# Mixer of a Trainium2 backbone layer: S5 scans of a pair of groups in one scan per direction, and mixer products moved from GpSimd to VectorE

## The chip, the core and the metric

The kernel runs on one core of one Trainium2 chip. The metric is the device time of one execution in microseconds (us), the median of several runs.

## What is computed

The program is one layer of a diffusion backbone: a half-step SwiGLU feed-forward block, a mixer, and a second feed-forward block, on 1024 latent tokens of width 1024 with 256 context tokens as a prefix. The change is in the mixer. There the width is split: one half goes through a gated short convolution on a grid, the other through a bidirectional S5 state-space scan, and both halves go into one output projection. The S5 part has 32 groups with 64 complex states each, in two directions. Cut to what matters:

```python
def s5_scan(ug, lam_bar, b_bar, h0, reverse):
    bu = jnp.einsum('blgh,gph->blgp', ug.astype(jnp.complex64), b_bar)
    first = bu.shape[1] - 1 if reverse else 0
    bu = bu.at[:, first].add(lam_bar * h0)
    a = jnp.broadcast_to(lam_bar, (1,) + bu.shape[1:])
    _, h = lax.associative_scan(_linear_recurrence, (a, bu), axis=1, reverse=reverse)
    return h
...
    st_c = s5_states(u_c, disc, (zero, zero))          # context tokens
    h0s = (st_c[0][:, -1], st_c[1][:, 0])
    p = modulate(rms_norm(x, mix_g_pre[i]), mods[3], mods[4]) @ w_in[i]
    bg, cg, v, u = jnp.split(p, splits, axis=-1)
    y_conv = bg * grid_short_conv(cg * v, conv_w[i])
    y_ssm = s5_readout(u, s5_states(u, disc, h0s), disc, ssm_d[i], w_glu[i], b_glu[i])
    y = jnp.concatenate([y_conv, y_ssm], axis=-1) @ w_out[i]
```

## The kernel before

The tokens of a sequence are taken in 128 chunks of 8 (CL = 128), so that a recurrence over 1024 tokens becomes one over 128 chunk states, and what lies inside a chunk is matrix products on TensorE. The 32 groups are worked in 16 pairs by the generator `s5_pair` (L1428 on); text below counts them from 0 to 15. The states of the forward direction stand on partitions 0 to 63, those of the backward direction on partitions 64 to 127.

For one pair the steps are these. TensorE forms the chunk inputs in PSUM (tiles `bt`, two groups, real and imaginary part, 128 latent chunks and 32 context chunks each). VectorE multiplies the context part with a table (four products of 128x64), adds and subtracts them, and sums them up to the start state (two reductions, written to column 0 or 127 of tile `w`). It then multiplies the latent part with a table of rotations (four products of 128x256 into `p1` and `p2`), and adds and subtracts (two of 128x256). The rotation makes the recurrence a real one with a coefficient `r8` that is constant for each state. So there are four real sequences of a direction (two groups, real and imaginary), and VectorE runs eight scans of 64x127, each with a start value taken from a column of `w`. At last the rotation is undone: two products of 128x512 and two sums of 128x256, which the kernel before gives to GpSimd (`pl`). The result `q1` is the operand of the pair's readout, matrix products that TensorE adds into the PSUM tiles `yps` of four pairs.

Around the pairs runs `cover`: units of the convolution branch (`conv`: twelve column blocks of `w_in`, each projected by 2 x 24 matrix products of 128x512) and of `out_conv`. The loop in `run` starts the chunk inputs of pair a+1, the VectorE part of pair a, some units of cover by the list `UNITS`, and the readout of pair a-1. The exact order on each engine is made by the scheduler at build time; each engine then works its list strictly in order. A projection in fp32 precision is three products of a high and a low part of the weights, which are split by `wcols` and `split` (L157): ScalarE writes the high part, a second engine subtracts it. The tables `PC` and `V0` say which of the convolution's splits and products go to GpSimd:

```python
nxt = self.wcols(win, seq[p + 1], nc.gpsimd if PC[p % len(PC)] else None)
...
if n == 2 and V0[j] or n == 1 and V1[j]:
    h_ = self.t2()
    nc.scalar.activation(h_, pt, AF.Copy)
    self.mul(t[:, cs], t[:, cs], h_, nc.gpsimd)
else:
    self.mul(t[:, cs], t[:, cs], pt)
```

Since GpSimd takes its operand from SBUF here, ScalarE copies the product out of PSUM first. After four pairs `s5_out` writes their readout to DRAM (`yd`), gathers it in eight loads and runs the gelu on it, on VectorE and ScalarE. Scratch tiles of the mixer come from a ring of twelve (`t2`).

Of the kernel before, what the change touches and what calls it, by code (L numbers as in the profile page):

```python
# [12 lines left out]
AF = mybir.ActivationFunctionType  # L13
OP = mybir.AluOpType
AX = mybir.AxisListType

P = 128
# [11 lines left out]
CL = NT // T8  # L29
# [39 lines left out]
class Kernel:  # L69
# [110 lines left out]
    def setup(self):  # L180
        nc, i = self.nc, self.i
        self.cp = self.pool("cp")
        self.dr = self.pool("dr", space=bass.MemoryType.DRAM)
        self.psum = self.pool("psum", bufs=8, space=bass.MemoryType.PSUM)
        self.sm = self.pool("sm", bufs=8)
        self.wp = self.pool("wp", bufs=6)
        self.tp = self.pool("tp", bufs=1)
        self.tb = self.t(self.tp, [P, 5 * D], "tb")
        self.ring([self.tb[:, D * k : D * k + D] for k in range(5)])
        self.wrs = [self.t(self.wp, [P, D], f"wr{k}", bufs=1) for k in range(4)]  # L190
        self.zp = self.pool("zp", bufs=32)

        dr = self.dr
        self.x1d = self.t(dr, [T8, CL, D], "x1d")
        self.x2d = self.t(dr, [T8, CL, D], "x2d")
        self.rowd = [self.t(dr, [KT, P], f"rowd{k}") for k in range(4)]
        self.pd = self.t(dr, [PAIRS, P, TO], "pd")
        self.pwd = self.t(dr, [P, D], "pwd")
        self.brd = self.t(dr, [P, D], "brd")
        self.gd = self.t(dr, [H, G, 15, H], "gd")  # L200
        self.td = self.t(dr, [P, G, P], "td")
        self.ud = self.t(dr, [G * H, T8, CL], "ud")
        self.ucd = self.t(dr, [G * H, T8, CC], "ucd")
        self.yd = self.t(dr, [T8, H, G, CL], "yd")
        self.zd = [self.t(dr, [P, NT], f"zd{k}") for k in range(4)]
        self.t2d = [self.t(dr, [P, 512], f"t2d{k}") for k in range(NF // 2)]
        self.scd = [self.t(dr, [P, 4 * NC], f"scd{k}") for k in range(6)]
        self.sd = [[self.t(dr, [P, NT], f"sd{n}_{k}") for k in range(NF)] for n in range(2)]

        cp = self.cp  # L210
        rows = self.t2([16, P])
        self.load(rows[0:8, :], i["c"][0].rearrange("(k p) -> k p", p=P))
        self.load(rows[8:16, :], i["c_ctx"].rearrange("(k p) -> k p", p=P))
        self.ident = self.t(cp, [P, P], "ident")
        make_identity(self.tc.nc, self.ident)
        srow = self.t2([16, P])
        nc.scalar.activation(srow, rows, AF.Silu)
        pt = self.ps()
        self.tr(pt[:, :16], srow, 16)
        self.scol = self.t(cp, [P, 16], "scol")  # L220
        nc.vector.tensor_copy(self.scol, pt[:, :16])
        self.ones = self.t(cp, [P, 1], "ones")
        nc.gpsimd.memset(self.ones, 1.0)
        self.modc = {}

    def selector(self):

        nc, cp = self.nc, self.cp
        red = self.t(cp, [P, 32], "red")
        nc.vector.tensor_reduce(  # L230
            red, self.ident.rearrange("p (a j) -> p j a", j=32), axis=AX.X, op=OP.add
        )
        self.sel = self.t(cp, [P, P], "sel")
        for a in range(4):
            nc.vector.tensor_copy(self.sel[:, 32 * a : 32 * a + 32], red)
# [1192 lines left out]
    def s5_pair(self, a, u, yps):  # L1428

        nc, pl = self.nc, self.nc.gpsimd  # L1430
        fw, bw = slice(0, 64), slice(64, 128)
        pa, pb = self.z([P, EO]), self.z([P, EO])
        self.load(pa, self.pd[a, :, :EO])
        self.load(pb[:, : TO - EO], self.pd[a, :, EO:])
        self.load(
            pb[:, TO - EO : PW - EO].rearrange("p (q n) -> p q n", q=2), self.td[:, 2 * a : 2 * a + 2, :]
        )
        yield
        us = [u[:, 2 * a + q, :] for q in range(2)]
        bm = lambda q, r: pa[:, BO + 256 * r + P * q : BO + 256 * r + P * q + P]  # L1440
        tab = lambda o, n: pb[:, o - EO : o - EO + 2 * n].rearrange("p (q c) -> p q c", q=2)
        bt = [self.ps()[:, : 2 * (CL + CC)].rearrange("p (r c) -> p r c", r=2) for _ in range(2)]
        for q in range(2):
            for r in range(2):
                nc.tensor.matmul(bt[q][:, r, :], bm(q, r), us[q], start=True, stop=True)

        hs = self.t2([P, 2, 2, 2, CC])
        shp = [P, 2, CC]
        for r in range(2):
            for q in range(2):  # L1450
                self.mul(
                    hs[:, r, q], bt[q][:, :, CL:], tab(FO + 64 * r, CC)[:, q].unsqueeze(1).to_broadcast(shp)
                )
        self.sub(hs[:, 0, :, 0], hs[:, 0, :, 0], hs[:, 1, :, 1])
        self.add(hs[:, 0, :, 1], hs[:, 0, :, 1], hs[:, 1, :, 0])
        w = self.t2([P, 2, 2, CL])
        for r, c in ((fw, 0), (bw, CL - 1)):
            nc.vector.tensor_reduce(w[r, :, :, c : c + 1], hs[r, 0], axis=AX.X, op=OP.add)

        shp = [P, 2, 2, CL]  # L1460
        er, ei = (tab(EO + 256 * r, CL) for r in range(2))
        p1, p2 = self.t2(shp), self.t2(shp)
        for q in range(2):
            for p, e in ((p1, er), (p2, ei)):
                self.mul(p[:, q], bt[q][:, :, :CL], e[:, q].unsqueeze(1).to_broadcast([P, 2, CL]))
        er, ei = (e.unsqueeze(2).to_broadcast(shp) for e in (er, ei))
        self.add(p1[:, :, 0], p1[:, :, 0], p2[:, :, 1])
        self.sub(p1[:, :, 1], p1[:, :, 1], p2[:, :, 0])
        n = CL - 1
        for q in range(2):  # L1470
            for r in range(2):
                for d, z, o, c in ((fw, slice(0, n), slice(1, CL), 0), (bw, slice(n, 0, -1), slice(n - 1, None, -1), n)):
                    r8 = self.r8[d, 2 * a + q : 2 * a + q + 1].to_broadcast([64, n])
                    nc.vector.tensor_tensor_scan(
                        w[d, q, r, o], r8, p1[d, q, r, z], w[d, q, r, c : c + 1], op0=OP.mult, op1=OP.add
                    )
        q1 = self.t2(shp)
        self.mul(q1, w, er, pl)
        self.mul(w, w, ei, pl)
        self.sub(q1[:, :, 0], q1[:, :, 0], w[:, :, 1], pl)  # L1480
        self.add(q1[:, :, 1], q1[:, :, 1], w[:, :, 0], pl)
        yield
        if not yps:
            yps.extend(self.ps() for _ in range(2))
        for q in range(2):
            o = yps[q][:, (a % 4) * CL : (a % 4) * CL + CL]
            t0 = TO - EO + P * q
            nc.tensor.matmul(o, pb[:, t0 : t0 + P], us[q][:, :CL], start=True, stop=False)
            for r in range(2):
                c0 = CO + 256 * r + P * q  # L1490
                nc.tensor.matmul(o, pa[:, c0 : c0 + P], q1[:, q, r, :], start=False, stop=r == 1)
        yield
# [26 lines left out]
    def conv(self, hi, lo, yc):  # L1519
# [5 lines left out]
        for p, c0 in enumerate(seq):  # L1525
# [5 lines left out]
            for h in range(2):  # L1531
# [3 lines left out]
                if h == 0 and p + 1 < len(seq):  # L1535
                    nxt = self.wcols(win, seq[p + 1], nc.gpsimd if PC[p % len(PC)] else None)
                if n == 0:
                    nc.scalar.activation(cv[:, cs], pt, AF.Copy)
                else:
                    t = cv if n == 1 else o  # L1540
                    if n == 2 and V0[j] or n == 1 and V1[j]:
                        h_ = self.t2()
# [70 lines left out]
    def run(self):  # L1613
# [41 lines left out]
        go = lambda tokens: [act[c]() for c in tokens]  # L1655
        go(S0)
        ab = (self.modc[1, 0], self.modc[0, 0])
# [357 lines left out]


PP = PH = PU = 0
PC = (0, 1, 0, 0, 1, 0, 1, 1, 0, 1, 1, 1)
FIVE = 4
S0 = 'lffllfllflllllll'  # L2020
S1 = 'wahhaahaahafPpaaqwhafpahpwhwhhwqqqqqqqqqqqqpqqqqPeePhhhPhhhhehPhhpewwhhhPPPphPwhhehPh'
S2 = 'hhhhhhhhhhhhpphhppppphp'
X2A = (0, 2)
FW3 = 18
V0 = (1, 1, 0, 0)
V1 = (0, 0, 0, 0)
UNITS = (5, 0, 0, 2, 0, 0, 1, 1, 2, 0, 2, 1, 1, 0, 3, 1, 0, 0, 6)

# [58 lines left out]
```

## Time and profile before

| | us |
|---|---|
| median of 3 runs (2123.9 to 2125.89) | 2124.05 |
| the profiled execution's own time | 2125.93 |
| its span, first to last instruction | 2124.2 |
| busy: TensorE (PE) | 1925.3 (91%) |
| busy: VectorE (DVE) | 1636.0 (77%) |
| busy: ScalarE (ACT) | 817.0 (38%) |
| busy: GpSimd (POOL) | 229.5 (11%) |

The profile is one execution, so the shares are averages over stages with different limits. The mixer's scans lie between 1122.4 and 1299.7 us of the span. The profile of this kernel names line 51 for nearly every instruction, since a helper records them all, so groups are told apart by the tiles that they write and read: `ps` is PSUM, `t` a scratch tile of the ring, `wr` a raw weight block and `w` its split, `z` a larger tile.

### The profile page before, as it was taken

What the parts mean: (1) busy time and instruction counts of PE and PEld (TensorE: products, weight loads), DVE (VectorE), ACT (ScalarE), POOL (GpSimd) and SP (SyncE); (2) the same over time, 40 slices, a digit from 0 to 9 for tenths busy, and PEclk for the clock granted to TensorE, in tenths of its full rate; (3) what the DMA queues carried; (4) which work ended last, traced back from release to release, by engine and by line L of the source; (5) the groups of instructions that cost most, each with busy time, mean ns of one, the idle gap of its engine ahead of it and who ended that gap; (6) DMA issues with size and microseconds to landing.
All of it is one profiled execution on the core that took longest, in us unless ns stands there. A gap on an engine that the chain in (4) does not pass through costs nothing.

```text
span 2124.2 us, 25468 instructions
## 1 busy us (share of the span) xinstructions
PE 1925.3 (91%) x9018; PEld 1594.7 (75%) x9018; DVE 1636.0 (77%) x2813; ACT 817.0 (38%) x1416; POOL 229.5 (11%) x136
## 2 busy tenths in 40 slices
PE   5779998898899988999997779998899999998997
PEld 4568776686899866877886668886688888886876
DVE  6689998998766699598549998478875555579867
ACT  5433322333343333566531113347233333333543
POOL 0000000041337100000003552010000000000000
PEclk9889999999999999999999899999899999999999
DMA  8347552344579969367684433233552322267754
GB/s 299 95 145 245 160 184 84 88 150 139 172 241 264 320 226 339 128 229 279 186 235 174 153 127 114 72 104 114 182 175 79 99 80 90 70 226 250 243 169 168
DMA packets 338444, 366.21 MB, mean 172 GB/s; under 512 B 43216, under 2 KB 250764, under 8 KB 338316
## 3 DMA queue, kind: packets, MB, share of 16 engines
q1 hardware_dynamic: 336012, 356.19, 51.6%
q10 hardware_dynamic: 2304, 8.39, 1.0%
q8 instruction: 71, 1.16, 0.2%
q14 instruction: 57, 0.47, 0.1%
HBM read 299.22 MB, written 67.35 MB: 173 GB/s over the span
## 4 chain that ended last, share of the span: by engine, by line
PE 54%; DVE 29%; DMA 8%; issue 4%; ACT 2%; POOL 2%; SPq 1%; DVEq 0%; ACTq 0%; POOLq 0%
PE ps L51 54%; DVE t L51 10%; DVE z L51 6%; DVE w L51 5%; DVE tb L51 5%; DMA wr<-in_ffn_w_down 2%; DMA tb<-in_w_ada 2%; POOL z L51 1%; SPq L51 1%; DMA wr<-in_ffn_w_gu 1%; DMA z<-in_w_ada 1%; ACT z L51 1%; ACT w L51 1%; DMA wr<-t2d 1%; ACT t L51 0%
## 5 line engine op out<-in xcount | busy, mean ns | idle before, releaser
L51 PE MATMUL ps<-z,w 128*128 128x512 f32 (+1 forms) x5712 | 1245.9, 379 | 94.4 <-ACT w L51 46.1
L51 PEld LDWEIGHTS ps<-z,w 128*128 128x128 f32 x5712 | 1020.8, 194 | 296.1 <-ACT w L51 52.5
L51 PE MATMUL ps<-w,w 128*128 128x512 f32 x1848 | 439.3, 397 | 29.9 <-DVE w L51 23.9
L51 PEld LDWEIGHTS ps<-w,w 128*128 128x128 f32 x1848 | 348.4, 191 | 117.5 <-DVE w L51 35.0
L51 ACT ACTIVATE w<-wr 128x512 fp32r<-128x512 f32 (+1 forms) x308 | 228.9, 747 | 378.8 <-PE ps L51 287.0
L51 DVE TENSOR_TENSOR w<-wr,w 128x512 fp32r<-128x512 f32 (+1 forms) x302 | 268.6, 894 | 91.1 <-ACT w L51 83.6
L51 ACT ACTIVATE w<-t 128x512 fp32r<-128x512 f32 x264 | 160.2, 626 | 294.0 <-DVE t L51 255.6
L51 DVE TENSOR_TENSOR w<-t,w 128x512 fp32r<-128x512 f32 x264 | 181.1, 699 | 40.9 <-ACT w L51 40.6
L51 DVE TENSOR_TENSOR t<-t,ps 128x512 f32<-128x512 f32 x150 | 102.2, 683 | 66.0 <-PE ps L51 65.6
L51 ACT ACTIVATE w<-z 128x512 fp32r<-128x512 f32 x132 | 83.3, 631 | 161.1 <-PE ps L51 158.4
L51 DVE TENSOR_TENSOR w<-z,w 128x512 fp32r<-128x512 f32 x132 | 90.8, 688 | 48.0 <-ACT w L51 47.8
L51 ACT ACTIVATE t<-ps 128x512 f32<-128x512 f32 (+2 forms) x135 | 73.7, 548 | 99.7 <-PE ps L51 98.0
L51 DVE TENSOR_TENSOR z<-z,z 128x512 fp32r<-128x512 f32 (+3 forms) x127 | 103.8, 852 | 9.6 <-ACT z L51 5.8
L51 DVE SCALAR_TENSOR_TENSOR tb<-tb,scol 128x1024 f32<-128x1024 f32 x77 | 97.9, 1280 | 8.6 <-DMA tb<-in_w_ada 8.4
L51 DVE TENSOR_TENSOR t<-wr 128x512 f32<-128x512 f32 x126 | 85.4, 685 | 16.7 <-DMA wr<-in_ffn_w_gu 11.1
L51 POOL TENSOR_TENSOR z<-z,z 128x1024 f32<-128x1024 f32 x24 | 85.4, 3576 | 76.4 <-PE ps L51 39.8
L51 ACT ACTIVATE t<-z 128x1024 bf16<-128x1024 f32 (+3 forms) x132 | 75.2, 605 | 44.3 <-DVE z L51 32.1
L51 ACT ACTIVATE t<-t 128x512 f32<-128x512 f32 (+1 forms) x81 | 50.6, 625 | 104.1 <-DVE t L51 100.1
L51 PE MATMUL ps<-z,t 128*128 128x512 f32 x384 | 87.8, 389 | 1.1 <-ACT t L51 1.1
L51 PEld LDWEIGHTS ps<-z,t 128*128 128x128 f32 x384 | 72.0, 188 | 16.4 <-ACT t L51 1.5
L51 POOL TENSOR_TENSOR tb<-tb 128x512 f32<-128x512 f32 x24 | 33.8, 1422 | 451.3 <-DVE w L51 431.0
L51 ACT ACTIVATE z<-z 128x512 fp32r<-128x512 f32 (+2 forms) x76 | 47.9, 672 | 78.6 <-DVE z L51 72.5
(124 smaller groups left out, 1447.6 us busy)
## 6 DMA issues: line engine op xcount, KB each, us to landing
wr<-in_ffn_w_gu SPq DMA_DIRECT2D x156, 512.0 KB, 4.1
wr<-in_ffn_w_down SPq DMA_DIRECT2D x242, 256.0 KB, 4.4
tb<-in_w_ada SPq DMA_DIRECT2D x64, 512.0 KB, 5.0
sd<-z SPq DMA_DIRECT2D x44, 512.0 KB, 4.8
z<-sd SPq DMA_DIRECT2D x88, 256.0 KB, 5.6
z<-in_w_ada SPq DMA_DIRECT2D x24, 512.0 KB, 6.1
wr<-in_ffn_w_down SPq DMA_DIRECT2D x22, 512.0 KB, 3.6
wr<-in_w_in SPq DMA_DIRECT2D x20, 512.0 KB, 4.0
```

What stands on the lines that cost most here:

```text
L51: r = f(*a, **kw)
```

## The change

The four sequences of a direction are laid end to end in one row of 516 columns, 129 for each sequence: a start state and 128 inputs. A coefficient tile `co` holds `r8` in every column but those between two sequences, where it holds 0, so that one scan runs through all four and begins anew at each. There are now two scans of 64x515 in a pair, one for each direction. ScalarE writes `co` for each pair, out of a constant `mask`, in two instructions of 128x258 and 128x259. The four operations after the scan go from GpSimd to VectorE. With `PC` and `V0` zero, six weight splits and four products of the convolution go to VectorE too, and the four copies out of PSUM on ScalarE that fed those products are gone. A pair takes six scratch tiles (`hs`, `pp`, `w`, `co`, `p2`, `q1`) and no longer five.

```diff
--- before.py
+++ after.py
@@ -222,6 +222,9 @@
         self.ones = self.t(cp, [P, 1], "ones")
         nc.gpsimd.memset(self.ones, 1.0)
         self.modc = {}
+        self.mask = self.t(cp, [P, 2 * CL + 3], "mask")
+        nc.gpsimd.memset(self.mask, 1.0)
+        nc.gpsimd.memset(self.mask[:, :: CL + 1], 0.0)
 
     def selector(self):
 
@@ -1453,32 +1456,39 @@
                 )
         self.sub(hs[:, 0, :, 0], hs[:, 0, :, 0], hs[:, 1, :, 1])
         self.add(hs[:, 0, :, 1], hs[:, 0, :, 1], hs[:, 1, :, 0])
-        w = self.t2([P, 2, 2, CL])
-        for r, c in ((fw, 0), (bw, CL - 1)):
-            nc.vector.tensor_reduce(w[r, :, :, c : c + 1], hs[r, 0], axis=AX.X, op=OP.add)
-
+
+
+        n = CL + 1
+        pp, w, co = self.t2([P, SW]), self.t2([P, SW]), self.t2([P, SW])
+        for q in range(2):
+            nc.scalar.activation(
+                co[:, 2 * n * q : 2 * n * (q + 1) + q], self.mask[:, : 2 * n + q], AF.Copy,
+                scale=self.r8[:, 2 * a + q : 2 * a + q + 1],
+            )
+        seg = lambda v, c: v[:, c : c + 4 * n].rearrange("p (q r c) -> p q r c", q=2, r=2)
+        for d, c in ((fw, 0), (bw, n)):
+            nc.vector.tensor_reduce(seg(pp, 0 if c == 0 else 1)[d, :, :, c - (c > 0) : c + (c == 0)], hs[d, 0], axis=AX.X, op=OP.add)
         shp = [P, 2, 2, CL]
         er, ei = (tab(EO + 256 * r, CL) for r in range(2))
-        p1, p2 = self.t2(shp), self.t2(shp)
+        p1, p2 = seg(pp, 0)[:, :, :, 1:], self.t2(shp)
         for q in range(2):
             for p, e in ((p1, er), (p2, ei)):
                 self.mul(p[:, q], bt[q][:, :, :CL], e[:, q].unsqueeze(1).to_broadcast([P, 2, CL]))
         er, ei = (e.unsqueeze(2).to_broadcast(shp) for e in (er, ei))
         self.add(p1[:, :, 0], p1[:, :, 0], p2[:, :, 1])
         self.sub(p1[:, :, 1], p1[:, :, 1], p2[:, :, 0])
-        n = CL - 1
-        for q in range(2):
-            for r in range(2):
-                for d, z, o, c in ((fw, slice(0, n), slice(1, CL), 0), (bw, slice(n, 0, -1), slice(n - 1, None, -1), n)):
-                    r8 = self.r8[d, 2 * a + q : 2 * a + q + 1].to_broadcast([64, n])
-                    nc.vector.tensor_tensor_scan(
-                        w[d, q, r, o], r8, p1[d, q, r, z], w[d, q, r, c : c + 1], op0=OP.mult, op1=OP.add
-                    )
-        q1 = self.t2(shp)
-        self.mul(q1, w, er, pl)
-        self.mul(w, w, ei, pl)
-        self.sub(q1[:, :, 0], q1[:, :, 0], w[:, :, 1], pl)
-        self.add(q1[:, :, 1], q1[:, :, 1], w[:, :, 0], pl)
+        nc.vector.tensor_tensor_scan(
+            w[fw, 1 : 4 * n], co[fw, : 4 * n - 1], pp[fw, : 4 * n - 1], 0.0, op0=OP.mult, op1=OP.add
+        )
+        nc.vector.tensor_tensor_scan(
+            w[bw, 4 * n - 1 : 0 : -1], co[bw, 4 * n : 1 : -1], pp[bw, 4 * n : 1 : -1], 0.0, op0=OP.mult, op1=OP.add
+        )
+        w = seg(w, 1)[:, :, :, :CL]
+        q1, q2 = self.t2(shp), p2
+        self.mul(q1, w, er)
+        self.mul(q2, w, ei)
+        self.sub(q1[:, :, 0], q1[:, :, 0], q2[:, :, 1])
+        self.add(q1[:, :, 1], q1[:, :, 1], q2[:, :, 0])
         yield
         if not yps:
             yps.extend(self.ps() for _ in range(2))
@@ -2015,14 +2025,15 @@
 
 
 PP = PH = PU = 0
-PC = (0, 1, 0, 0, 1, 0, 1, 1, 0, 1, 1, 1)
+PC = (0,)
 FIVE = 4
+SW = 520
 S0 = 'lffllfllflllllll'
 S1 = 'wahhaahaahafPpaaqwhafpahpwhwhhwqqqqqqqqqqqqpqqqqPeePhhhPhhhhehPhhpewwhhhPPPphPwhhehPh'
 S2 = 'hhhhhhhhhhhhpphhppppphp'
 X2A = (0, 2)
 FW3 = 18
-V0 = (1, 1, 0, 0)
+V0 = (0, 0, 0, 0)
 V1 = (0, 0, 0, 0)
 UNITS = (5, 0, 0, 2, 0, 0, 1, 1, 2, 0, 2, 1, 1, 0, 3, 1, 0, 0, 6)
 
```

In the built order this is what stands on VectorE for pair 3, from its first product to its scans (`ps_9386` and `ps_9387` are its chunk inputs; the built program names a scan SCALAR_TENSOR_TENSOR). Before:

```order
L51 TENSOR_TENSOR t_1449_9392<-ps_9386,z_9271 128x64
L51 TENSOR_TENSOR t_1449_9392<-ps_9387,z_9271 128x64
L51 TENSOR_TENSOR t_1449_9392<-ps_9386,z_9271 128x64
L51 TENSOR_TENSOR t_1449_9392<-ps_9387,z_9271 128x64
L51 TENSOR_TENSOR t_1449_9392<-t_1449_9392 128x2x32 x2
L51 TENSOR_REDUCE t_1450_9399<-t_1449_9392 64x4 x2
L51 TENSOR_TENSOR t_1451_9402<-ps_9386,z_9271 128x256
L51 TENSOR_TENSOR t_1452_9403<-ps_9386,z_9271 128x256
L51 TENSOR_TENSOR t_1451_9402<-ps_9387,z_9271 128x256
L51 TENSOR_TENSOR t_1452_9403<-ps_9387,z_9271 128x256
L51 TENSOR_TENSOR t_1451_9402<-t_1451_9402,t_1452_9403 128x2x128 x2
L51 SCALAR_TENSOR_TENSOR t_1450_9399<-r_91_175,t_1450_9399,t_1451_9402 64x127 x8
```

With the change, from the two scans of the pair ahead (`ps_9376` and `ps_9377` are now pair 3's chunk inputs, `t_1440` is the `q1` of pair 2):

```order
L51 SCALAR_TENSOR_TENSOR t_1437_9284<-t_1438_9285,t_1436_9283 64x515 x2
L51 TENSOR_TENSOR t_1440_9299<-t_1437_9284,z_9217 128x512
L51 TENSOR_TENSOR t_1439_9290<-t_1437_9284,z_9217 128x512
L51 TENSOR_TENSOR t_1451_9382<-ps_9376,z_9266 128x64
L51 TENSOR_TENSOR t_1451_9382<-ps_9377,z_9266 128x64
L51 TENSOR_TENSOR t_1451_9382<-ps_9376,z_9266 128x64
L51 TENSOR_TENSOR t_1451_9382<-ps_9377,z_9266 128x64
L51 TENSOR_TENSOR t_1440_9299<-t_1440_9299,t_1439_9290 128x2x128 x2
L51 TENSOR_TENSOR t_1451_9382<-t_1451_9382 128x2x32 x2
L51 TENSOR_REDUCE t_1452_9389<-t_1451_9382 64x4 x2
L51 TENSOR_TENSOR t_1452_9389<-ps_9376,z_9266 128x2x128
L51 TENSOR_TENSOR t_1455_9396<-ps_9376,z_9266 128x256
```

The two products of the pair ahead stand directly behind its scans, its two sums behind the first four products of pair 3, and the eight scans are two.

On TensorE this is the place of pair 13's readout before (`ps_10309` and `ps_10310` are the readout's PSUM tiles, `t_1563` and `t_1574` the `q1` of pairs 12 and 13, `ps_10322` a chunk input of pair 14, `ps_10361` a unit of the convolution with 24 products):

```order
L51 MATMUL ps_10309<-t_1563_10151,z_10035 128x128 x2
L51 MATMUL ps_10310<-tb_72,z_10036 128x128
L51 MATMUL ps_10310<-t_1563_10151,z_10035 128x128 x2
L51 MATMUL ps_10309<-tb_72,z_10115 128x128
L51 MATMUL ps_10309<-t_1574_10213,z_10114 128x128 x2
L51 MATMUL ps_10310<-tb_72,z_10115 128x128
L51 MATMUL ps_10322<-tb_72,z_10176 128x160 x2
L51 MATMUL ps_10323<-tb_72,z_10176 128x160 x2
L51 MATMUL ps_10361<-z_7420,w_10273 128x512 x2
L51 MATMUL ps_10361<-z_7420,w_10274 128x512
```

With the change the readout of pair 13 reads `t_1585`, and stands here (`ps_10311` is that unit of the convolution, of which the last products are shown, `ps_10348` and `ps_10349` are the chunk inputs of pair 15):

```order
L51 MATMUL ps_10311<-z_7429,w_10227 128x512
L51 MATMUL ps_10311<-z_7430,w_10226 128x512 x2
L51 MATMUL ps_10311<-z_7430,w_10227 128x512
L51 MATMUL ps_10348<-tb_72,z_10270 128x160 x2
L51 MATMUL ps_10262<-t_1585_10166,z_10073 128x128
L51 MATMUL ps_10263<-t_1585_10166,z_10073 128x128
L51 MATMUL ps_10349<-tb_72,z_10270 128x160 x2
```

The first half of pair 13's readout moved from before the convolution's 24 products to behind them, and behind the chunk inputs of pair 14 and half of those of pair 15.

On ScalarE the coefficient tiles stand between other work; `t_1558` to `t_1583` are those of pairs 11 to 13, with the mixer's own steps around them:

```order
L51 ACTIVATE z_8494<-z_8497 128x1024
L51 ACTIVATE z_8494<-z_8494 128x1024
L51 ACTIVATE t_1558_10017<-mask_175,r_92_178 128x258
L51 ACTIVATE t_1558_10017<-mask_175,r_92_178 128x259
L51 ACTIVATE t_1571_10093<-mask_175,r_92_178 128x258
L51 ACTIVATE t_1571_10093<-mask_175,r_92_178 128x259
L51 ACTIVATE w_10337<-wr_2_73 128x1024
L51 ACTIVATE z_10119<-ps_9917 128x4x128
L51 ACTIVATE z_10119<-ps_9918 128x4x128
L51 ACTIVATE t_1583_10152<-mask_175,r_92_178 128x258
L51 ACTIVATE t_1583_10152<-mask_175,r_92_178 128x259
```

Four coefficient instructions stand behind the two steps on `z_8494`, which belong to the gelu of the second four pairs; before, nothing on VectorE's scans depended on ScalarE's list.

## Rows read from the trace of the kernel before

**Rows 1.** The page: span, and busy time of three engines with share and instructions.

```profile
span 2124.2 us, 25468 instructions
...
PE 1925.3 (91%) x9018; PEld 1594.7 (75%) x9018; DVE 1636.0 (77%) x2813; ACT 817.0 (38%) x1416; POOL 229.5 (11%) x136
```

**Rows 2.** Engines by stretch: the scans, and what follows; columns in the first line.

```profile
core 0: us, PE busy (x) PEld busy (x) DVE busy (x) ACT busy (x) POOL busy (x), PEclk, DMA share, GB/s
1122.40:1299.70 177.30, 139.43 (x687) 118.53 (x687) 169.36 (x382) 26.31 (x43) 87.90 (x69) 0.90 0.39 131
...
1310.00:1373.30 63.30, 63.30 (x280) 52.08 (x278) 34.82 (x52) 26.73 (x47) 0.00 (x0) 1.00 0.34 108
```

**Rows 3.** Waits, 1122.4 to 1299.7: us in total, times, longest.

```profile
PE ps L51 <- POOL t L51: 26.6, 8, 7.7
...
PE ps L51 <- DVE t L51: 5.1, 2, 3.6
...
DVE z L51 <- DMA z<-yd: 1.3, 1, 1.3
```

**Rows 4.** The chain that ended last, around the last stall: start, us, what.

```profile
1270.58 0.49 DVE t L51
...
1271.14 1.27 POOL t L51
...
1272.48 2.32 POOL t L51
...
1278.12 21.96 PE ps L51 x105
```

**Rows 5.** VectorE by shape, 1122.4 to 1299.7: xcount, busy us, mean ns, idle before.

```profile
L51 DVE TENSOR_TENSOR_SCAN t<-r,t,t 64x127 f32<-64x127 f32 x128 | 63.5, 496 | 1.6
...
L51 DVE TENSOR_TENSOR t<-t,t 128x256 f32<-128x256 f32 x32 | 20.9, 693 | 0.5
L51 DVE TENSOR_TENSOR t<-t 128x64 f32<-128x64 f32 x32 | 15.1, 512 | 0.5
...
L51 DVE SCALAR_TENSOR_TENSOR z<-z,cols,z 128x1024 f32<-128x1024 f32 x3 | 5.3, 1762 | 1.3 <-DMA z<-yd 1.3
L51 DVE TENSOR_TENSOR z<-z,ps 128x512 f32<-128x512 f32 x6 | 4.0, 681 | 0.1
L51 DVE SCALAR_TENSOR_TENSOR z<-z,cols,z 128x960 f32<-128x960 f32 x2 | 3.9, 1954 | 0.0
L51 DVE TENSOR_TENSOR w<-wr,w 128x1024 fp32r<-128x1024 f32 x2 | 3.5, 1767 | 0.0
```

**Rows 6.** VectorE in order of time, pairs 14 and 15: start, us, instructions.

```profile
1283.87 0.36 DVE L51 TENSOR_TENSOR t<-t 128x64 f32<-128x64 f32 x2
...
1286.39 0.76 DVE L51 TENSOR_TENSOR t<-t,t 128x256 f32<-128x256 f32 x2
...
1291.67 0.90 DVE L51 TENSOR_TENSOR t<-t 128x64 f32<-128x64 f32 x2
...
1294.67 1.18 DVE L51 TENSOR_TENSOR t<-t,t 128x256 f32<-128x256 f32 x2
```

**Rows 7.** VectorE by shape, whole span.

```profile
L51 DVE TENSOR_TENSOR t<-z,z 128x512 f32<-128x512 f32 x44 | 30.0, 685 | 0.1
...
L51 DVE SCALAR_TENSOR_TENSOR z<-z,sy,tb 128x1024 f32<-128x1024 f32 x24 | 29.8, 1283 | 0.3
...
L51 DVE TENSOR_TENSOR z<-wr,z 128x1024 fp32r<-128x1024 f32 x8 | 9.6, 1220 | 0.7 <-ACT z L51 0.7
...
L51 DVE TENSOR_TENSOR tb<-tb 128x64 f32<-128x64 f32 x16 | 3.4, 222 | 0.2
```

**Rows 8.** TensorE in order of time, around the last stall.

```profile
1276.46 0.80 PE L51 MATMUL ps<-t,z 128*128 128x128 f32 x2 [7.68 <-POOL t L51]
...
1281.08 6.37 PE L51 MATMUL ps<-z,w 128*128 128x512 f32 x24
```

**Rows 9.** GpSimd in order of time: its work of pairs 13 and 14.

```profile
1271.14 3.66 POOL L51 TENSOR_TENSOR t<-t,z 128x512 f32<-128x512 f32 x2 [3.80 <-DVE t L51]
...
1291.07 2.66 POOL L51 TENSOR_TENSOR t<-t,z 128x512 f32<-128x512 f32 x2 [9.78 <-DVE t L51]
```

**Rows 10.** ScalarE by shape, whole span: an activation near the size of a coefficient instruction.

```profile
L51 ACT ACTIVATE t<-ps 128x256 f32<-128x256 f32 x26 | 9.4, 367 | 2.5 <-PE ps L51 2.5
```

## The prediction

> **What bounds the kernel now.** I read the page first. TensorE is busy for 91% of the span and VectorE for 77% [rows 1], so over the whole program TensorE comes first. The change lies in one stage, so I then took the engines by stretch. Between 1122.4 and 1299.7 us, the stretch of the sixteen pairs, VectorE is busy for 169.4 of 177.3 us and TensorE for only 139.4, so TensorE stands idle for 37.9 us; between 1310 and 1373.3 us it is TensorE that is busy all the time [rows 2]. VectorE sets the pace of the scans, and TensorE that of what follows. Third come the waits of that stretch: TensorE waits longest for GpSimd, 26.6 us in eight waits, since its readout of a pair needs the four GpSimd operations behind the scans; it waits 5.1 us for VectorE's tiles, and VectorE itself hardly waits, 1.3 us for the gather of `yd` [rows 3]. Last the chain of the end: it runs through VectorE's scans up to 1271.07 us, then 7 us through GpSimd's operations of pair 13, and at 1278.12 us passes to TensorE, which works on from there [rows 4]. So a microsecond saved ahead of 1278 counts if it brings pair 13's readout forward; one saved behind it on VectorE or GpSimd is hidden under TensorE.
>
> **The scans.** The 128 scans of 64x127 take 63.5 us, 496 ns each [rows 5]. No row shows a scan of 515 columns. From below: one that costs as an ordinary product does, where 512 columns take 685 ns and 64 take 222, that is 1.03 ns a column and 156 ns fixed [rows 7]; the 388 columns more then bring a scan to 496 + 388 x 1.03 = 0.90 us. From above: nothing is fixed and all of the 496 ns goes with the columns, 3.9 ns each, 2.01 us. Between them I take the parts. Fixed are 156 ns, and a column operand costs some 60 more (1283 against 1220 ns for 1024 columns with and without it [rows 7]). This leaves 280 ns for 127 columns, 2.2 ns each, and 515 columns with 156 ns make 1.29 us. All 32 come to 41.3 us: 22.2 us less than before.
>
> [...]
>
> **The products.** Each pair gives VectorE two products of 128x512 at 685 ns [rows 7] and two sums of 128x256, which took 0.76 us together where GpSimd was idle [rows 6]: 2.13 us, 34.1 us for the 16. In both orders they stand behind the pair's own scans, so this lies on VectorE's path, with no cover.
>
> **The convolution's part.** Five splits fall into the stretch (the sixth lies ahead of it, where VectorE waits anyway): at 1.22 us [rows 7] they take 6.1 us. Four products out of PSUM at 0.68 us [rows 5] take 2.7. The four copies that ScalarE loses save nothing, as ScalarE is busy 26.3 of 177.3 us [rows 2].
>
> **What VectorE gets back.** While GpSimd works, VectorE's operations on two SBUF tiles take longer. At 1283.87 us, with GpSimd idle, the two sums of 128x64 took 0.36 us and those of 128x256 0.76; eight us later, beside GpSimd's products of pair 14, the same took 0.90 and 1.18 [rows 6, 9]. Over the stretch the small sums cost 15.1 us where 16 x 0.36 = 5.8 would do, the larger 20.9 in place of 12.2 [rows 5, 6]: 18.0 us too much. The taps' 1024 columns (three at 1762 ns against 1283), their 960 columns (two at 1954, some 1220 by the same measure) and two splits (1767 against 1220) add 4.0 [rows 5, 7]. With GpSimd silent in the stretch I count all 22.0 us back.
>
> [...]
>
> **The sum.** Over the stretch VectorE's work changes by -22.2 + 34.1 + 8.8 - 22.0 = -1.3 us, next to nothing. What counts is the point of the last stall. Up to the end of pair 13's operations there are 14 pairs: scans -19.4, products +29.8; relief on the sums -17.1 (pair 14 had none to give, pair 15 0.96) and some -2.5 elsewhere; five splits and three products +8.1; and two taps and gelu steps, which stood behind pair 13's scans and now stand before its products, +2.5. That is +1.4: pair 13's `q1` is ready on VectorE at 1271.1 + 1.4 = 1272.5 us, where TensorE got its second part at 1278.12 [rows 4, 8]. So TensorE goes on 5.6 us earlier. Besides, the 24 convolution products that it ran behind this readout, 6.4 us [rows 8], now stand ahead of it and can fill the wait. If TensorE has come so far by then, the gain is 12.0 us; if it stands at an earlier readout all that time, 5.6. It has 37.9 us of idle time to draw on, but its other waits follow VectorE's pace, so I take the middle, 9 us. The span goes to 2124.2 - 9 = 2115. The profiled execution took 2125.9, and so would take 2117; the median of the runs shown is 1.9 us below it, and I forecast 2115 for the median.
>
> **Edits at no cost.** The 32 coefficient instructions on ScalarE, about 0.37 us each [rows 10], make 11.7 us beside 26.3 busy of 177.3 [rows 2]. The cover is gone if they stand late in ScalarE's list: it works in order, and several of them are behind steps that wait for TensorE or for the gelu of the four pairs before. VectorE's scan then waits, with all of its list behind it, and TensorE's readout too. By the order there are about two pairs of VectorE work between such a step and the scan, some 16 us. The sixth scratch tile of a pair leaves the ring of twelve holding two pairs; a tile comes free when TensorE has read the `q1` of two pairs ago. The two memsets of `mask` lie at the start. No DMA is added.
>
> **Next in line.** The gelu's first step on VectorE waits for the gather of `yd`, 1.3 us in all now [rows 3]. With GpSimd's delay gone from the loop, VectorE meets it sooner, and it stands between pair 13's scans and products. Up to 2 us more at this place are in the range.
>
> **Rivals.**
> - TensorE drains further: the wait for pair 13 is filled and shorter waits go with it. From scans of 0.90 us, 28 x 0.39 = 10.9 us earlier, and the full 12: 23 us, 2101. Against it speaks TensorE's own 139.4 us [rows 2]. Chance 0.15.
> - The gain is absorbed, by late coefficients, the gather and the ring: 5.6 less 2 for the gather and about 2 for one late scan, 2122, no change that can be told. For it speaks that VectorE's own sum is so near zero. Chance 0.18.
> - The scan's cost goes with the columns, 2.01 us. Up to pair 13 that is 28 x 0.72 = 20.2 us more, and 2124.2 - 9 + 20.2 = 2135: slower. It decides from 1.29 + 9/28 = 1.61 us a scan. Against it speaks the 156 ns that every form of rows 7 has fixed. Chance 0.09.
> - The relief doesn't come, because the longer sums have another cause than GpSimd. Then 2115 + 19.6 = 2135. Against it stands pair 14 [rows 6, 9]. [...] Chance 0.05.
>
> **How the numbers follow.** The forecast, 2109 to 2119, has 0.53. About 0.2%, 4.2 us, is what a measurement of this kernel can tell from no change. Faster are the forecast and the first rival, less a little of the forecast's upper edge: 0.67. The second rival and that edge make "the same", 0.19, the last two "slower", 0.14. The range of 2103 to 2127 leaves out the end of the first rival and most of the slower cases; its top is 2115 with scans at 1.5 us (28 x 0.21 = 5.9), the conv products not filling (3.2) and 2 to 3 us of waits.
>
> **What would show it.** Scans of 64x515 near 1.3 us, 32 of them; sums of 128x64 at 0.36 us a pair throughout, and of 128x256 at 0.76; no wait of TensorE for GpSimd between 1122 and 1300; VectorE's busy time in the stretch about as before; TensorE continuous from 1266 to 1273 us on. Wrong would be a scan above 1.6 us, sums as long as before, or VectorE waiting for ScalarE ahead of scans for more than a few us.

## The result, and the profile after

The changed kernel takes 2137.69 us in the median of nine runs (2129.89 to 2139.64); the kernel before, run beside it, takes 2125.72. The ratio is 1.0052, with a 95% interval of 1.0036 to 1.0067: slower by 0.5%, some 12 us, where 2115 was forecast. The profiled execution below took 2129.89 us, the shortest of the nine, so its rows show less of the loss than the median.

The page: span, and busy time of the engines.

```profile
span 2128.0 us, 25361 instructions
...
PE 1937.4 (91%) x9018; PEld 1587.9 (75%) x9018; DVE 1623.4 (76%) x2791; ACT 828.6 (39%) x1444; POOL 134.0 (6%) x64
```

The stage of the pairs by engine (against [rows 2]).

```profile
core 0: us, PE busy (x) PEld busy (x) DVE busy (x) ACT busy (x) POOL busy (x), PEclk, DMA share, GB/s
1122.40:1299.70 177.30, 154.03 (x778) 132.03 (x777) 168.90 (x385) 44.40 (x83) 0.00 (x0) 0.93 0.45 145
```

VectorE by shape in the same stage (against [rows 5]).

```profile
L51 DVE TENSOR_TENSOR_SCAN t<-t,t 64x515 f32<-64x515 f32 x32 | 39.2, 1224 | 1.0
L51 DVE TENSOR_TENSOR t<-t,t 128x256 f32<-128x256 f32 x64 | 25.6, 421 | 0.9
...
L51 DVE TENSOR_TENSOR t<-t,z 128x512 f32<-128x512 f32 x32 | 20.7, 688 | 0.5
...
L51 DVE TENSOR_TENSOR w<-wr,w 128x1024 fp32r<-128x1024 f32 x8 | 9.8, 1220 | 0.1
...
L51 DVE TENSOR_TENSOR z<-z,ps 128x512 f32<-128x512 f32 x13 | 8.8, 681 | 5.2 <-PE ps L51 5.2
...
L51 DVE TENSOR_TENSOR t<-t 128x64 f32<-128x64 f32 x32 | 5.7, 220 | 0.0
```

TensorE's waits in that stage (against [rows 3]; none for GpSimd is left).

```profile
PE ps L51 <- DVE z L51: 10.8, 2, 9.9
PE ps L51 <- DVE t L51: 9.7, 4, 3.8
PE ps L51 <- DMA z<-pd: 2.6, 1, 2.6
```

The stage does what was forecast of it: GpSimd silent, VectorE as busy as before, and TensorE idle for 177.3 - 154.0 = 23.3 us where it was 37.9, with 778 matmuls in the stretch where there were 687. The chain that ended last shows TensorE unbroken from 1265.67 us, and then one new stop, the gather of the last four pairs' readout. TensorE's own list has other work up to 1306.56 us; it then waits 4.44 us:

```profile
1265.67 30.68 PE ps L51 x152
1296.37 1.08 ACT z L51 x2
1297.48 3.63 DMA yd<-z
...
1304.59 2.67 DMA z<-yd
...
1307.39 3.56 DVE z L51 x3
```

```profile
1310.99 34.31 PE L51 MATMUL ps<-z,t 128*128 128x512 f32 x140 [4.44 <-DVE z L51]
```

So the gain is there. The loss is elsewhere. TensorE reaches the first matmuls of the scans (`ps<-tb,z`) at 1127.16 us, before at 1121.70, though its list up to there is the same (first the kernel before, then the changed one):

```profile
1121.70 4.18 PE L51 MATMUL ps<-tb,z 128*128 128x160 f32 x28
```

```profile
1127.16 3.87 PE L51 MATMUL ps<-tb,z 128*128 128x160 f32 x28
```

TensorE by stretch, first of the kernel before, then of the changed one, in two stretches of unchanged feed-forward work:

```profile
core 0: us, PE busy (x), PEclk, DMA share, GB/s
160.00:260.00 100.00, 99.32 (x441) 1.00 0.62 201
1700.00:1800.00 100.00, 100.00 (x443) 1.00 0.25 79
```

```profile
160.00:260.00 100.00, 100.00 (x435) 1.00 0.62 196
1700.00:1800.00 100.00, 100.00 (x432) 1.00 0.25 79
```

In the second stretch, at the full granted clock of 1.00 and without an idle moment, 443 matmuls in 100 us became 432: one takes 231 ns and no longer 226. In the first, where the kernel before idles for 0.7 us, 441 became 435. These rows, far from any changed instruction, are the start of the search.

### The profile page after: what moved, and what is told of

It is laid out like the page before. It is cut to its first block, busy times and chain, and to the rows that moved or that the text cites. A ratio compares the mean times of both kernels' runs of the same rounds, so it can differ in the third digit from the quotient of the medians.

```text
span 2128.0 us, 25361 instructions
## 1 busy us (share of the span) xinstructions
PE 1937.4 (91%) x9018; PEld 1587.9 (75%) x9018; DVE 1623.4 (76%) x2791; ACT 828.6 (39%) x1444; POOL 134.0 (6%) x64
## 4 chain that ended last, share of the span: by engine, by line
PE 55%; DVE 26%; DMA 9%; issue 4%; ACT 2%; POOL 2%; SPq 1%; DVEq 0%; ACTq 0%; POOLq 0%
PE ps L51 55%; DVE t L51 9%; DVE z L51 6%; DVE w L51 6%; DVE tb L51 4%; DMA tb<-in_w_ada 2%; POOL z L51 2%; DMA wr<-in_ffn_w_gu 2%; DMA wr<-in_ffn_w_down 1%; SPq L51 1%; DMA z<-in_w_ada 1%; ACT z L51 1%; ACT w L51 1%; ACT t L51 1%; DMA z<-sd 1%
## 5 line engine op out<-in xcount | busy, mean ns | idle before, releaser
L51 PEld LDWEIGHTS ps<-w,w 128*128 128x128 f32 x1848 | 347.7, 190 | 119.0 <-DVE w L51 34.1
L51 DVE TENSOR_TENSOR w<-wr,w 128x512 fp32r<-128x512 f32 (+1 forms) x308 | 276.1, 901 | 91.7 <-ACT w L51 85.5
L51 DVE TENSOR_TENSOR z<-t,ps 128x512 f32<-128x512 f32 (+1 forms) x52 | 29.6, 569 | 56.0 <-PE ps L51 55.0
L51 ACT ACTIVATE z<-ps 128x512 f32<-128x512 f32 x74 | 41.3, 594 | 68.9 <-PE ps L51 63.8
```

What stands on the lines that cost most here:

```text
L51: r = f(*a, **kw)
```

## The experiments

The theories were these. Of the memory places: the mask and the wider scratch tiles (`SW` = 520 columns) move every tile behind them, and matmuls everywhere pay. Of the work: the change's own instructions and their order cost the time. Distance below is the start of the first `z` tile less that of the first `w` tile in a partition's memory, as the program places them; before it is 73,728 bytes, a multiple of 256, and after the change 384 more, 12 scratch tiles by 32 bytes. The kernel before has 443 matmuls in the stretch of the last column.

| run | bytes more | us | before beside it | ratio, 95% | matmuls, 1700 to 1800 us |
|---|---|---|---|---|---|
| the change | 384 | 2137.69 | 2125.72 | 1.0052, 1.0036 to 1.0067 | 432 |
| b_shift32 | 0 | 2127.87 | 2123.23 | 1.0022, 1.0009 to 1.0035 | 443 |
| b_shift64 | 0 | 2127.11 | 2123.23 | 1.0018, 1.0005 to 1.0031 | 443 |
| a_pad32 | 384 | 2139.31 | 2123.23 | 1.0074, 1.0054 to 1.0093 | 431 |
| a_pad32_oldconv | 384 | 2137.56 | 2123.23 | 1.0064, 1.0044 to 1.0083 | 430 |
| b_layout | 384 | 2145.93 | 2122.48 | 1.0112, 1.0098 to 1.0126 | 430 |
| b_t520 | 384 | 2145.10 | 2122.48 | 1.0114, 1.0098 to 1.0129 | 430 |
| a_zrel | 1024 | 2117.55 | 2122.48 | 0.9982, 0.9973 to 0.9992 | 443 |
| b_z384 | 384 | 2141.85 | 2122.34 | 1.0094, 1.0064 to 1.0124 | 431 |
| a_zrel_last | 1024 | 2112.42 | 2122.34 | 0.9947, 0.9929 to 0.9965 | 443 |
| a_zrel_scan | 1024 | 2116.07 | 2122.34 | 0.9976, 0.9961 to 0.9991 | 443 |
| b_z128 | 128 | 2136.63 (one run) | 2122.34 | | 431 |
| b_z256 | 256 | 2121.33 (one run) | 2130.17 | | 443 |
| b_z512 | 512 | 2120.58 (one run) | 2130.17 | | 443 |
| b_z64 | 64 | 2128.68 (one run) | 2118.64 | | 439 |
| b_z32 | 32 | 2146.19 (one run) | 2118.64 | | 430 |

### All tiles shifted together

The kernel before with a pad among the constants (16 columns for 64 bytes); a_pad32 puts the same 8 columns ahead of the mask in the changed kernel.

```diff
+        self.pad = self.t(cp, [P, 8], "pad")
+        nc.gpsimd.memset(self.pad, 1.0)
```

> The kernel before, with one unused tile of 8 columns (32 bytes a partition) put among the constants, so that every large tile of the on-chip memory begins 32 bytes behind a multiple of 64 bytes, as the wr, w, tb, gate and z tiles do after the change; every engine's list is that of before. Theory of the memory places (the 259-column mask and the 520-column tiles move all tiles, and the matmuls everywhere pay for it): the matmuls z<-w between 1036 and 1070 us and those of the last 300 us of full TensorE take 2 to 2.5% longer, and the time is 8 to 16 us above before (ratio 1.004 to 1.0075). Theory of the work (the moved products and the order of the mixer's lists cost the time): nothing moves, ratio 0.999 to 1.001.

> As the run with 32 bytes, with 16 columns (64 bytes) instead of 8, so that the large tiles begin at multiples of 64 bytes again, though not of 512. Theory of the memory places with 64 bytes as the step that matters: ratio 0.999 to 1.001. If it is a larger step (128 to 512 bytes) that matters: as slow as with 32 bytes, ratio 1.004 to 1.0075. Theory of the work: ratio 0.999 to 1.001 in either case.

> The changed kernel, with the same unused 32 bytes ahead of the mask, so that the wr, w, tb, gate and z tiles begin at multiples of 64 bytes; the lists of the engines are those of the changed kernel. Theory of the memory places: the 2 to 2.5% of the matmuls come back, the mixer's gain of about 10 us of TensorE idle time stays, and the time is 6 to 12 us below before (ratio 0.994 to 0.997). Theory of the work: as the changed kernel, ratio 1.004 to 1.007.

The theory as it stood fell: 32 and 64 bytes leave 443 matmuls, and the changed kernel on multiples of 64 bytes is as slow as without (431 matmuls against 432). The two shifts cost 0.2% all the same, for which their profiles show no cause (spans of 2121.7 and 2123.2 us, no longer than before); that stays open. But all kernels with the change were at 430 to 432. What they had and the shifts lacked was the distance between tiles.

### The convolution's work

```diff
-PC = (0,)
+PC = (0, 1, 0, 0, 1, 0, 1, 1, 0, 1, 1, 1)
-V0 = (0, 0, 0, 0)
+V0 = (1, 1, 0, 0)
```

> The run before this one with the convolution's products and the splits of w_in divided between GpSimd and VectorE as before the change (PC and V0 of before), so that of the change only the scans and the rotation's products on VectorE are left. If the move of the convolution's work is what costs the mixer its time: 4 to 10 us below the run before this one. If the relief of VectorE from GpSimd's company carries the gain, as the prediction has it: 3 to 10 us above it, since 24 VectorE operations of 0.7 us go but GpSimd slows VectorE's sums and taps again.

Neither came: 1.0064 lies within the interval of a_pad32. As far as these intervals tell (each 0.2% either way), moving the convolution's products and splits to VectorE neither costs nor carries the gain. The work moved is ten operations, six splits and four products, and not the 24 of the expectation.

### The places without the work

b_t520 has the first edit alone, b_layout both. One wide tile is enough for the first: all twelve places of the ring take the size of the widest. The lists of TensorE and VectorE are those of before, instruction by instruction.

```diff
-        rows = self.t2([16, P])
+        rows = self.t2([P, 520])[:16, :P]
...
+        self.pad = self.t(cp, [P, 259], "pad")
+        nc.gpsimd.memset(self.pad, 1.0)
```

> The kernel before with the places in memory of the changed kernel and none of its work: an unused tile of 259 columns stands where the mask stands, and the 12 work tiles are 520 columns wide though 512 are used. The engines' lists are those of before. Found so far: at the granted clock of 1.00 the last matmuls run at 443 to 445 in 100 us in the kernel before and with its tiles shifted by 32 or 64 bytes, and at 430 to 434 in the three kernels with the change. Theory of the memory places (now: the distance between the stationary and the moving operand's tiles, 384 bytes more than before, not the start of all tiles): 430 to 434 matmuls here too, and the time 14 to 22 us above before (ratio 1.007 to 1.010). Theory of the work (the change's own instructions cost the time and the slower matmuls come of something else in its program): 443 to 445, ratio 0.998 to 1.003.

> The kernel before with only the 12 work tiles 520 columns wide (the tiles behind them, gate and z, lie 384 bytes further, wr, w and tb stay). Theory of the distance: as the run with the whole layout, 430 to 434 matmuls in 100 us, ratio 1.006 to 1.010. If the mask's 1,056 bytes matter instead: 443 to 445 and ratio 0.999 to 1.002. Theory of the work: the same as before.

This settles it: without one changed instruction in the mixer, the places cost 1.1%, 23.5 us, and since b_t520 costs 22.6, it is the width of the scratch tiles and not the mask. TensorE by operation over the whole span, first before, then b_layout (count, busy us, mean ns, idle before):

```profile
L51 PE MATMUL ps<-z,w 128*128 128x512 f32 (+1 forms) x5712 | 1245.9, 379 | 94.4 <-ACT w L51 46.1 <-ACT z L51 16.7 <-DVE w L51 15.9
L51 PE MATMUL ps<-w,w 128*128 128x512 f32 x1848 | 439.3, 397 | 29.9 <-DVE w L51 23.9 <-ACT w L51 4.3 <-DVE z L51 1.0
```

```profile
L51 PE MATMUL ps<-z,w 128*128 128x512 f32 (+1 forms) x5712 | 1270.7, 383 | 91.8 <-ACT w L51 45.8 <-ACT z L51 16.5 <-DVE w L51 13.0
L51 PE MATMUL ps<-w,w 128*128 128x512 f32 x1848 | 438.3, 396 | 29.0 <-DVE w L51 22.0 <-ACT w L51 5.3 <-DVE z L51 1.0
```

The reader is to see the pair of rows: matmuls that read one operand from `z` and one from `w` take 24.8 us more, most of the 27.0 by which TensorE's busy time grows (1925.3 to 1952.3 us); those that read both from `w`, whose places to each other are unchanged, take no more (438.3 us against 439.3). The medians lie 23.5 us apart, the two traces 17.3, so the match with the loss is a rough one.

### The distance put right, and varied

```diff
+        self.gap = self.t(self.pool("gp"), [P, 160], "gap")
         self.zp = self.pool("zp", bufs=32)
...
-        red = self.t(self.cp, [P, 32], f"red{mod}_{cond}")
+        red = self.t(self.cp, [P, 32], "reds", bufs=2)
...
```

> The changed kernel with 640 unused bytes between the work tiles and the z tiles, so that w and z tiles lie a multiple of 1,024 bytes apart again (before: of 4,096); to make room, nine small sums of the modulation share two places. The lists are those of the changed kernel. Theory of the distance: 443 to 445 matmuls in 100 us, and with the mixer's gain the time is 4 to 12 us below before (ratio 0.994 to 0.998). If the distance isn't the cause, or counts by 4,096 bytes: 430 to 434, ratio 1.004 to 1.008. Theory of the work: ratio 1.004 to 1.008.

The b_z runs put the same kind of gap into the kernel before (8 to 128 columns).

> The kernel before with 384 unused bytes between the gate tile and the z tiles: the work tiles keep their 512 columns and their places, and only the z tiles lie further from the w tiles by what the 520-column tiles moved them. Theory of the distance between z and w: 430 to 434 matmuls in 100 us and ratio 1.009 to 1.013, as with the whole layout (1.011). If it is the work tiles' own width or start that slows the kernel: 443 to 445, ratio 0.999 to 1.002.

> As the run before it with 128 unused bytes instead of 384. Looked at for the number of matmuls in 100 us alone. If any distance that isn't a multiple of 512 bytes costs: 430 to 434. If 128 bytes are a step that does no harm: 443 to 445.

> The kernel before with 256 unused bytes ahead of the z tiles. Looked at for the number of matmuls in 100 us (fast 443 to 445, slow 430 to 434). If every distance that isn't a multiple of 512 bytes costs: 430 to 434. If 256 bytes are the step: 443 to 445.

> The kernel before with 512 unused bytes ahead of the z tiles. If the distance counts by 512 bytes or less: 443 to 445 matmuls in 100 us. If only multiples of 1,024 bytes are fast: 430 to 434.

> The kernel before with 64 unused bytes ahead of the z tiles. Looked at for the number of matmuls in 100 us (fast 443 to 445, slow 430 to 434). If every distance between w and z that isn't a multiple of 256 bytes costs: 430 to 434. If only the odd multiples of 128 bytes (128 and 384, the slow ones so far) cost: 443 to 445.

> As the run before it with 32 bytes: 430 to 434 if every distance off the multiples of 256 bytes costs, 443 to 445 if only the odd multiples of 128 do.

With the distance at a multiple of 1,024 bytes the changed kernel is faster than before, at 443 matmuls; moving the `z` tiles alone by 384 bytes makes the kernel before as slow as the whole layout does, within the intervals. By the counts 256 and 512 bytes are free (443), 32, 128 and 384 cost (430 to 431), and 64 costs a third of it (439). Neither expectation for 64 bytes came. Of the single runs only the counts are read.

The traces hold a second and a third pair of operands that tell the same. The 384 matmuls `ps<-z,t` read `z` and scratch tiles. In the order below they are those of the kernel before, of b_z64, of b_z384 and of a_zrel_last, in which the `z` tiles lie at a multiple of 1,024 bytes from the `w` tiles, but ten of the twelve scratch tiles, 2,080 bytes each, lie at no multiple of 256 bytes from either:

```profile
L51 PE MATMUL ps<-z,t 128*128 128x512 f32 x384 | 87.8, 389 | 1.1 <-ACT t L51 1.1
L51 PE MATMUL ps<-z,t 128*128 128x512 f32 x384 | 88.7, 392 | 1.1 <-ACT t L51 1.1
L51 PE MATMUL ps<-z,t 128*128 128x512 f32 x384 | 90.0, 395 | 1.1 <-ACT t L51 1.1
L51 PE MATMUL ps<-z,t 128*128 128x512 f32 x384 | 89.9, 395 | 1.1 <-ACT t L51 1.1
```

So one and the same kernel, a_zrel_last, runs `ps<-z,w` at the fast rate (443 in 100 us) and `ps<-z,t` at the slow one (395 ns). The matmuls `ps<-w,t` read no `z` tile. Seventy of them in a row take 16.17 us before and in b_z384, where only `z` moved, and 16.52 or 16.53 in every kernel with 520-column scratch tiles (the kernel before, then the changed one):

```profile
1003.56 16.17 PE L51 MATMUL ps<-w,t 128*128 128x512 f32 x70
```

```profile
1005.89 16.52 PE L51 MATMUL ps<-w,t 128*128 128x512 f32 x70
```

In these runs each pair is slow where its own two operands lie off a multiple of 256 bytes, and nowhere else. It follows that a_zrel is not wholly repaired: by these rows the scratch tiles cost it some 3 us still, an estimate (2.1 us of `ps<-z,t`, and 264 matmuls `ps<-w,t` at 5 ns).

### Where the rest of the gain went

```diff
         wo = [self.wrows(self.i["w_out"][0], k * P, zr) for k in range(4)]
+        self.wlast = self.last
...
-        next(outs.pop())
+        with self.tc.issue_after(self.wlast):
+            next(outs.pop())
```

> The changed kernel with the z tiles a multiple of 1,024 bytes from the w tiles (as in the run a_zrel, 0.998) and the last group's skip and GELU, which wait for the gather of yd, put behind the splits of w_out's first four blocks on VectorE. Theory that part of the mixer's gain is given back at its end, where VectorE stands 9.1 us at z<-yd with those splits behind it and TensorE then waits 4.3 us for one: that wait goes, and the time is 3 to 6 us below a_zrel (ratio to before 0.995 to 0.997). If TensorE or VectorE is held up again right behind it: as a_zrel, 0.997 to 0.9995.

It came, and a little more. VectorE in order of time in a_zrel: it stands 9.08 us at the gelu's first step, and the splits of w_out, `z<-wr,z`, are behind it; for the first of them TensorE then waits 4.31 us.

```profile
1301.54 2.41 DVE L51 SCALAR_TENSOR_TENSOR z<-z,cols,z 128x1024 f32<-128x1024 f32 x2 [9.08 <-DMA z<-yd]
1303.87 1.22 DVE L51 TENSOR_TENSOR z<-wr,z 128x1024 fp32r<-128x1024 f32 x1
```

```profile
1305.15 20.22 PE L51 MATMUL ps<-z,t 128*128 128x512 f32 x74 [4.31 <-DVE z L51]
```

In a_zrel_last all four splits run while the gather is under way, and of its wait 0.47 us is left:

```profile
1293.17 1.22 DVE L51 TENSOR_TENSOR z<-wr,z 128x1024 fp32r<-128x1024 f32 x1
...
1295.43 2.35 DVE L51 TENSOR_TENSOR z<-wr,z 128x1024 fp32r<-128x1024 f32 x2
...
1298.90 1.22 DVE L51 TENSOR_TENSOR z<-wr,z 128x1024 fp32r<-128x1024 f32 x1
1300.59 1.29 DVE L51 SCALAR_TENSOR_TENSOR z<-z,cols,z 128x1024 f32<-128x1024 f32 x1 [0.47 <-DMA z<-yd]
```

This version beats both kernels: 2112.42 us, 0.5% below before.

### The scan alone

a_zrel with the rotation's four operations on GpSimd (`pl` as their last argument, as before) and the old `PC` and `V0`.

```diff
-        self.mul(q1, w, er)
-        self.mul(q2, w, ei)
+        self.mul(q1, w, er, pl)
+        self.mul(q2, w, ei, pl)
...
```

> As a_zrel, with the rotation's products, the convolution's products and the splits on GpSimd as before the change: only the long scan is left of the change. If the scan's 22 us on VectorE make the gain and the moves to VectorE only exchange one load for another (the step 'relief' of the prediction cancels): ratio 0.994 to 0.998, as fast as a_zrel or faster. If freeing GpSimd is needed for the gain, since TensorE waited for GpSimd 26.6 us: slower than a_zrel by 3 us or more, ratio 0.999 to 1.003.

As fast as a_zrel (0.9976 and 0.9982, the intervals overlap), so the moves off GpSimd cancel. Its trace shows both ways come out alike in the stage. From 1115 to 1330 us TensorE waits for GpSimd nearly as long as before, and VectorE's sums are slow beside it, 820 ns for 128x64 in place of 220.

```profile
PE ps L51 <- POOL t L51: 21.4, 7, 5.6
```

```profile
L51 DVE TENSOR_TENSOR t<-t 128x64 f32<-128x64 f32 x32 | 25.0, 820 | 0.5
```

In a_zrel TensorE waits for VectorE in place of GpSimd. From 1115 to 1290 us it idles for 37.9 us before, 25.7 in a_zrel and 26.6 in a_zrel_scan (the rows in this order, columns as in the stage's row above):

```profile
1115.00:1290.00 175.00, 137.13 (x673) 116.50 (x672) 164.59 (x364) 26.00 (x32) 83.89 (x65) 0.90 0.44 149
1115.00:1290.00 175.00, 149.28 (x766) 127.99 (x765) 168.35 (x383) 41.98 (x78) 0.00 (x0) 0.94 0.47 152
1115.00:1290.00 175.00, 148.43 (x744) 127.36 (x743) 164.97 (x305) 44.71 (x84) 86.95 (x73) 0.92 0.45 152
```

## Why the prediction was wrong

**The failed step is "Edits at no cost".** It counted the instructions of the new tiles and asked whether twelve of them still hold two pairs. It did not count that a tile of 520 columns moves whatever is allocated behind it. That edit alone costs 22.6 us (b_t520; 23.5 with the mask in b_layout), in matmuls that the change doesn't touch. No rival had it, and the range of 2103 to 2127 didn't reach the result. The coefficient instructions, which it did count, held nothing up: in the stage VectorE waits for ScalarE once, 1.8 us, and not at a scan.

**Scans: right.** 1224 ns where 1.29 us was taken, an estimate from [rows 5, 7], and 39.2 us for all where 41.3 was.

**Products: right.** 20.7 us and half of the 25.6 us of 64 sums are 33.5, against 34.1.

**The convolution's part: mis-sized.** 8 splits stand in the stage against 2, and 13 products against 6: 6 x 1.22 + 7 x 0.68 = 12.1 us, not 8.8. TensorE gets further in the stage, 778 matmuls and not 687, and brings more of this work into it.

**What VectorE gets back: right.** The small sums went from 15.1 to 5.7 us (5.8 forecast), the older half of the larger from 20.9 to 12.8 (12.2).

**The sum: right in kind, mis-sized, and its reason not borne out.** VectorE's busy time went from 169.4 to 168.9 us. TensorE goes on unbroken from 1265.67 us, at the edge of the 1266 to 1273 forecast, and pair 13's two sums end on VectorE at 1273.1 us, where 1272.5 was forecast:

```profile
1272.35 0.76 DVE L51 TENSOR_TENSOR t<-t,t 128x256 f32<-128x256 f32 x2
```

But the stage began 5.5 us late, so this agreement is luck. In a_zrel, which enters it at 1121.99 us, the same sums end at 1268.1: against the 1271.1 from which the forecast counts, the path came out 3 us shorter and not 1.4 longer. The scans are 1.9 us of that (14 of 16 parts of 24.3 us are 21.3, not 19.4); the rest wasn't traced. With the distance repaired the change gains 2122.48 - 2117.55 = 4.9 us, about half of the 9 forecast. Two terms that the sum lacked stand against it: the 3 us, by the estimate above, that the scratch tiles still cost, and TensorE's 4.3 us at the last gather. With that wait covered the gain is 2122.34 - 2112.42 = 9.9 us, but this has an edit in it that the forecast did not have. And the prediction put the gain down to GpSimd's delay, while the scan alone gives as much with that delay in place.

**Next in line: wrong place.** The prediction meant the gather of the third four pairs, 1.3 us, between pair 13's scans and products. There VectorE no longer waits at all. The wait that counts is the gather of the last four pairs, which the prediction left out: 9.4 us on VectorE and 4.4 on TensorE (9.1 and 4.3 in a_zrel), with the splits queued behind it. VectorE waited there before too, 8.1 - 1.3 = 6.8 us (its gathers from 1110 to 1330 us in the first row), but TensorE had work all the while (second row):

```profile
L51 DVE SCALAR_TENSOR_TENSOR z<-z,cols,z 128x1024 f32<-128x1024 f32 x4 | 6.6, 1643 | 8.1 <-DMA z<-yd 8.1
```

```profile
1300.00:1350.00 50.00, 50.00 (x226) 41.55 (x225) 32.92 (x59) 21.87 (x43) 4.20 (x4) 1.00 0.41 136
```

**Open.** At the slow distance the work of the change gains more than at the fast one: 1.0052 and 1.0074 against 1.0112 and 1.0114 is 0.4 to 0.6%, against 0.18% in a_zrel. Some 0.15% of this is the scratch tiles' 3 us, which b_layout and b_t520 pay too, but the kernel before, beside a_zrel, doesn't. a_zrel also lets nine small sums share two places, which no run tried alone. What the rest is no run here says. Why the distance matters to TensorE was not tried either.

## What to carry to other kernels

A scratch tile that grows moves all that is allocated behind it, so compare matmul counts at a granted clock of 1.00 in a stretch that the change doesn't touch (here 443 against 432 in 100 us) before explaining anything in the stretch that it does. A kernel with the new places and the old work separates the two in one run. And when an engine comes early to a wait, read what stands behind it in its list: here VectorE stood 9.1 us at the gather with four splits behind it, and these, moved ahead of that wait, were worth as much as the repaired change itself, some 5 us each.

## What the hardware showed

Not expected was how the rate of a matmul hung, in these runs, on where its two operands lay to each other. At a granted clock of 1.00, with one operand in `z` and one in `w`, 443 matmuls ran in 100 us at distances of 0, 256, 512 and 1,024 bytes more than 73,728, 439 at 64, and 430 to 432 at 32, 128 and 384. Shifting all tiles together by 32 or 64 bytes left 443, so it was not the start of a tile that counted. Two other pairs of operands, `z` with the scratch tiles and `w` with them, were slow where their own distance was off a multiple of 256 bytes (395 against 389 ns a matmul, 16.52 against 16.17 us for seventy), also in kernels where `z` and `w` ran at the fast rate.
